# Where the conditioning loads and transpositions stand in the first mixer of a two-layer decoder trunk

## The chip, the cores and the metric

The kernel runs on one core of one Trainium2 chip. Its five engines work side by side, each through a queue of its own, in order: TensorE (PE) multiplies matrices and transposes, VectorE (DVE) and ScalarE (ACT) do elementwise work, GpSimd (POOL) and SyncE (SP) here mostly begin DMA transfers. An instruction waits in its queue for semaphores of other engines or of transfers, and everything behind it in that queue waits with it. The metric is the device time of one execution in microseconds.

## The reference

Two layers of a decoder trunk, for 256 tokens of width 1024, in fp32. Each layer takes six vectors of 1024 numbers from the conditioning vector `c`: a shift, a scale and a gate for the mixer and for the ConvFFN.

```python
cond = jax.nn.silu(c)
for layer in range(DEPTH):
    mod = cond @ ada_w[layer] + ada_b[layer]
    shift_m, scale_m, gate_m, shift_f, scale_f, gate_f = [m[:, None, :] for m in jnp.split(mod, 6, axis=-1)]
    h = rmsnorm(x, mix_pre_g[layer]) * (1.0 + scale_m) + shift_m
    if layer % 2 == 0:
        y = even_mixer(h, ab_w_in[i], ab_w_out[i], rel_bias)     # 8 MoBA heads "a", 8 dilated heads "b"
    else:
        y = odd_mixer(h, ...)                                    # latent attention, stick-breaking
    x = x + gate_m * rmsnorm(y, mix_post_g[layer])
    h = rmsnorm(x, ffn_pre_g[layer]) * (1.0 + scale_f) + shift_f
    y = conv_ffn(h, ffn_w_up[layer], ffn_conv_w[layer], ffn_conv_b[layer], ffn_w_down[layer])
    x = x + gate_f * rmsnorm(y, ffn_post_g[layer])
```

`even_mixer` multiplies `h` by `ab_w_in` into q, k, v of group a and of group b, adds a bias by distance to the scores of each head, takes softmaxes, and multiplies the heads' outputs by `ab_w_out`.

## The kernel before

Every fp32 product of weights and activations is made of three matmuls over a high and a low part. A weight tile is loaded (`load`, tag `raw`, four buffers), ScalarE casts its high part and VectorE subtracts it for the low part (`split`).

The first mixer runs in these stages. **Slices**: the inner dimension of 1024 is taken in four slices of 256. For each, the shift and scale of the mixer come from `ada_first` (its weights, `aw_first`, loaded by SP), `x` is transposed and conditioned, and q, k (`qk_mm`) and v (`v_mm`) of group a are accumulated. PE, DVE and ACT keep an order written out by hand here (`in_order`), up to `in_order.close()`. **Group a**: four pairs of heads (`attend`, tiles `sab`, `ltab`, `stab`, `oTab`). PE makes scores, VectorE adds the bias table `bt` and finds maxima (L590), ScalarE takes exponentials, VectorE scales (L601, L602), PE transposes (L604) and multiplies by v (L613, L616). **Projection b** (`qkv_proj`, tiles `psb`): weights `rawb_0`, `rawb_1` for q, the same names again for k, and `rawbv` for v. **Group b**, the same for the other eight heads, with tables of its own. **Output projection** (`y0m`), then the **first boundary**: gate, residual, norm, transposition, and the columns of scale and shift of the ConvFFN; then the ConvFFN of layer 0 (`u`), and layer 1.

The bias tables `bt` are read by SP out of `bias_d`, a table in DRAM that the kernel writes in the slices (L906), so `bt` waits for that write.

The other conditioning vectors are made in pieces of 512 columns beside this work. A piece is named by its first column among the 6144: 2048 and 2560 are the gate of the mixer, 3072 and 3584 the shift, 4096 and 4608 the scale, 5120 and 5632 the gate of the ConvFFN. Its four weight tiles `aw` (four buffers) are loaded by `ada_load`, all on POOL's queue. A piece of kind "p" is summed by PE (`ada_main`, 16 matmuls, L160). A piece of kind "v" is summed by VectorE (`ada_sum`, eight steps into `acc`, L207 and L205), in small steps handed out between other work by `step_aside`, and then transposed by four matmuls on PE (L177) and reduced by VectorE (`ada_keep`). In layer 0, 4096, 4608 and 3584 are of kind "v". `ADA_AT` says at which point each is requested: 2048 at "a0", 4096 at "a1", 2560 and 3072 at "a3", 4608 at "bv", 3584 at "b3". `gate_halves` starts the ConvFFN's gate at the boundary. Outside the hand-written order a scheduler sets each engine's order, by the order in which the code asks for things and by what each needs.

`tc.issue_after(...)` says behind which instruction a load may be put in its queue. A wait for a buffer that is still read is put in by the compiler. SP's transfers use eight semaphores in turn.

Of the kernel before, what the change touches and what calls it, by code (L numbers as in the profile page):

```python
# [17 lines left out]
P = 128  # L18
S = 256
D = 1024  # L20
# [23 lines left out]
    "dk": [("v", 1, 4, 1)],  # L44
    "d3": [("v", 1, 3, 1)],
}
BUFS = {"raw": 4, "whi": 4, "wlo": 4, "aw": 4, "gate": 2, "qkv": 8, "t": 13, "o": 8, "part": 2, "brow": 2,
        "ss": 4, "rstd": 4, "st": 4, "rp": 2, "kr": 2}


# [15 lines left out]
def trunk_kernel(  # L66
# [8 lines left out]
    nc = tc.nc  # L75
# [14 lines left out]
    def bank(name, tag="g"):  # L90
        return psum.tile([P, 512], F32, tag=tag, name=name, bufs={"g": 3, "a": 1}[tag])
# [43 lines left out]
    nc.vector.tensor_mul(cpad[:, :, 0], sil, cT)  # L135

    mods, last_load, last_gelu, last_full, last_h, last_down, last_low, last_main = {}, [], [], [], [], [], [], []
    last_rstd, last_slice, last_first = [], [], []

    def ada_load(layer, c0, tag="aw"):  # L140
        ws = []
        for u in range(4):
            w = tl(tag, [P, 2, 512], f"aw_{layer}_{c0}_{u}")
            with tc.issue_after(last_rstd[0].ins):
                last_load[:] = [nc.gpsimd.dma_start(  # L145
                    w, ada_w[layer, u * 256:(u + 1) * 256, c0:c0 + 512].rearrange("(k p) f -> p k f", p=P))]
            ws.append(w)
        return ws
# [22 lines left out]
    def ada_keep(layer, which, k0, ps, part, blocks, gain, per=4):  # L171

        n = len(blocks)
        dst = mods[layer, which][:, k0:k0 + n]
        cols = ps[:, blocks[0] * P:(blocks[-1] + 1) * P]
        for b in blocks:
            nc.tensor.transpose(ps[:, b * P:(b + 1) * P], part[:, b * P:(b + 1) * P], ident)  # L177
        nc.vector.tensor_reduce(dst, cols.rearrange("p (b j r) -> p b j r", j=per, r=P // per)[:, :, :, 0],
                                axis=mybir.AxisListType.X, op=ALU.add)
        b0 = layer * 48 + which * KT + k0  # L180
        nc.vector.tensor_add(dst, dst, vT[:, b0:b0 + n])
        if gain is not None:
            g0 = gain + layer * KT + k0
            nc.vector.scalar_tensor_tensor(dst, dst, 1.0, vT[:, g0:g0 + n], op0=ALU.add, op1=ALU.mult)

    aside = []

    def columns_for(layer, which):
        if (layer, which) not in mods:
# [2 lines left out]
    def step_aside(n=1):  # L192

        for _ in range(n):
            if aside:
                with tc.issue_after(last_low[0].ins):
                    if next(aside[0], aside) is aside:
                        aside.pop(0)
# [10 lines left out]
    def ada_vector(layer, which, h, gain):  # L209

        columns_for(layer, which)
        c0 = which * D + h * 512
        ws = ada_load(layer, c0)
        acc = small(f"acc_{layer}_{c0}", tag="part")
        yield from ada_sum(acc, ws)
        yield
        ada_keep(layer, which, 4 * h, bank(f"ada_{layer}_{c0}", "a"), acc, range(4), gain, P)

    def ada_cols(layer, which, h, gain=None):

# [31 lines left out]
    def ada_gate(layer, which, h, post_g, tag="aw", on="a", on_vector=False):  # L252

        c0 = which * D + h * 512
        ws = ada_load(layer, c0, tag)
        if (layer, which) not in mods:
            mods[layer, which] = tl("gate", [P, D], f"gate_{layer}_{which}")
            with tc.issue_after(last_load[0].ins):
                nc.gpsimd.dma_start(mods[layer, which], post_g[layer:layer + 1, :].broadcast_to([P, D]))
        g = mods[layer, which][:, h * 512:(h + 1) * 512]  # L260
        part = small(f"part_{layer}_{c0}", tag="brow")
        if on_vector:
            brow = small(f"brow_{layer}_{c0}", (1, 512), tag="t")
            nc.scalar.dma_start(brow, ada_b[layer:layer + 1, c0:c0 + 512])
            yield from ada_sum(part, ws)
            yield
            nc.vector.tensor_add(part[0:1, :], part[0:1, :], brow)
            ps = bank(f"ada_{layer}_{c0}", on)
            nc.tensor.matmul(ps, ones, part, start=True, stop=True)
            nc.vector.tensor_mul(g, ps, g)  # L270
            return
        nc.scalar.dma_start(part[P - 1:P, :], ada_b[layer:layer + 1, c0:c0 + 512])
        ps = bank(f"ada_{layer}_{c0}", on)
        yield
        ada_main(ps, ws, at_once=which == 2)
        yield
        nc.scalar.copy(part[0:P - 1, :], ps[0:P - 1, :])
        yield
        nc.tensor.matmul(ps, ones, part, start=True, stop=True)  # L279
        yield  # L280
        nc.vector.tensor_mul(g, ps, g)

    def gate_halves(which, layer, post_g):
        step_aside(99)
        halves = [ada_gate(layer, which, h, post_g, *on) for h, on in enumerate((("aw", "a"), ("qkv", "g")))]
        for h in halves:
            next(h)
        return halves
# [19 lines left out]

    def load(src, k, n, name):
        raw = tl("raw", [P, k, n], name)  # L310
        nc.sync.dma_start(raw, src.rearrange("(k p) f -> p k f", p=P))
        return raw

    def split(src, shape, name, aside=False, tags=("whi", "wlo")):
# [190 lines left out]
    def rows_of(w, u, c0, n, name):  # L505
        return load(w[u * 512:(u + 1) * 512, c0:c0 + n], 4, n, f"raw{name}_{u}")
# [10 lines left out]
                nc.scalar.copy(view, ps)  # L517
        return evac

    def qkv_proj(w, c0, name):  # L520

        q, k, v = qkv_tiles(name)
        list(qkv_steps(w, c0, name, q, k, v))
        return q, k, v

    def qkv_tiles(name):
        q, k, v = (qkv_tile(f"{n}{name}") for n in "qkv")
        return q, k, v.rearrange("p (t a) b -> p t (a b)", t=2)

    def qkv_steps(w, c0, name, q, k, v):  # L530
        for i, (dst, sc) in enumerate(((q, HD ** -0.5), (k, None))):
            ps = y_tile(f"ps{name}_{i}")
            for u in range(2):
                feat_mm([ps[:, 0, :], ps[:, 1, :]], rows_of(w, u, c0 + i * 512, 512, f"{name}{i}"), u, f"{name}{i}",
                        keep_feat(dst, sc) if u else None)
            more_ada(f"{name}{'qk'[i]}")
        yield
        ps = y_tile(f"ps{name}_v")
        for u in range(2):
            tok_mm([ps[:, 0, :], ps[:, 1, :]], rows_of(w, u, c0 + 1024, 512, f"{name}v"), u, 512, f"{name}v")  # L540
        keep_v(v, [ps[:, 0, :], ps[:, 1, :]])
        more_ada(f"{name}v")
# [248 lines left out]
    def slice_load(i):  # L791
        k0, n = SLICES[i]
        w = w_in[k0 * P:(k0 + n) * P]
        raw_qk[i] = tl("raw", [P, n, 1024], f"rawaqk_{i}")
        for k in range(n):
            nc.sync.dma_start(raw_qk[i][:, k, :], w[k * P:(k + 1) * P, 0:1024])
        raw_v[i] = tl("raw", [P, n, 512], f"rawav_{i}")
        last_slice[:] = [nc.sync.dma_start(raw_v[i], w[:, 1024:1536].rearrange("(k p) f -> p k f", p=P))]

    def slice_x(i, ts=range(2)):  # L800
        k0, n = SLICES[i]
# [118 lines left out]
        keep_feat(qkv[1])(half, pk[:, half, :])  # L920
    keep_v(qkv[2], pv)

    in_order.close()

    def pairs_ab(group, q, k, v):
# [4 lines left out]

    pairs = pairs_ab(0, *qkv)
    gs = attend(pairs, "a")
    qkv = qkv_proj(w_in, 1536, "b")
    gs += attend(pairs_ab(1, *qkv), "b")
    ys = y_tiles("y0m")
    out_proj(ys, ab_w_out[0], gs[0:4], True, False, "o0a")
# [215 lines left out]
```

## Time and profile before

| what | value |
|---|---|
| time, median of three runs | 699.66 us (698.59 to 701.04) |
| the profiled execution | 697.84 us, of which its span is 695.9 us |
| PE busy | 658.0 us, 95% of the span, 4541 matmuls |
| DVE busy | 526.7 us, 76% |
| ACT busy | 368.6 us, 53% |
| POOL busy | 95.2 us, 14% |
| DMA | 159.10 MB, 229 GB/s over the span |

Times in the rows are microseconds from the start of the span. A row of the timeline gives start, length, engine, line, operation, output and inputs, how many instructions it joins, and in brackets how long the engine had been idle before it and what ended that. PEclk is the TensorE clock that was granted, as a share of full speed. "q1 hardware_dynamic" is the queue of the transfers begun by SP (and ACT), "q0 software_dynamic" of those begun by POOL.

### The profile page before, as it was taken

To read this page: it belongs to the slowest core of one execution; us is meant where nothing else is said; L and a number is where in the kernel's file an instruction comes from. 1 tells how busy PE (TensorE), PEld (TensorE's weight loads), DVE (VectorE), ACT (ScalarE), POOL (GpSimd) and SP (SyncE) were. 2 spreads that over 40 slices of the span, in tenths; PEclk is the share of its full clock that TensorE was granted. 3 is DMA by queue.
4 is the path that set the end of the run, shared out by engine and by line. 5 is a ranking of instruction groups with operands and counts; after the bars stand their busy time and mean duration, and the time that the engine had idled before them with its cause. 6 is when DMAs were issued, how large, how long until landed. Compare 5 with 4: busy or idle time off the path is not lost.

```text
span 695.9 us, 11779 instructions
## 1 busy us (share of the span) xinstructions
PE 658.0 (95%) x4541; PEld 573.1 (82%) x4541; DVE 526.7 (76%) x1007; ACT 368.6 (53%) x644; POOL 95.2 (14%) x180
## 2 busy tenths in 40 slices
PE   7978999489999999999998999999999999999996
PEld 6856886367699999999996997767699999999994
DVE  2443784685889999999997886874788777777775
ACT  3323754454675555455655644785465555555552
POOL 2020212230301011111124012631200000000000
PEclk9998999879999999999999999999999999999999
DMA  9999987995578878778894858723256655555611
GB/s 312 295 378 253 368 298 248 301 307 209 178 243 269 259 261 303 257 260 287 270 340 142 303 184 295 224 85 108 90 182 211 200 195 182 182 182 183 187 55 61
DMA packets 90466, 159.10 MB, mean 229 GB/s; under 512 B 4087, under 2 KB 62483, under 8 KB 90411
## 3 DMA queue, kind: packets, MB, share of 16 engines
q1 hardware_dynamic: 78259, 114.24, 49.7%
q0 software_dynamic: 12128, 44.11, 18.7%
q8 instruction: 35, 0.57, 0.3%
q14 instruction: 20, 0.16, 0.1%
q10 hardware_dynamic: 24, 0.02, 0.0%
HBM read 156.52 MB, written 1.84 MB: 228 GB/s over the span
## 4 chain that ended last, share of the span: by engine, by line
PE 80%; DMA 9%; DVE 4%; ACT 3%; POOL 1%; issue 1%; SPq 0%; DVEq 0%; POOLq 0%; ACTq 0%
PE u L480 35%; PE y1f L701 9%; PE y0f L701 8%; DMA aw_first<-in_ada_w 5%; PE psb L480 3%; PE psd L480 3%; PE y0m L701 2%; PE y1m L701 2%; DMA rawav<-in_ab_w_in 2%; DMA bt<-bias_d 2%; PE ada L160 1%; PE sab L604 1%; PE ada_first L160 1%; ACT junknm L338 1%; PE sab L613 1%
## 5 line engine op out<-in xcount | busy, mean ns | idle before, releaser
L145 POOL DMA_DIRECT2D aw<-in_ada_w x80 | 58.2, 729 | 333.1 <-DVE acc L205 181.6
L750 ACT ACTIVATE cv<-u,cvT 128x256 f32<-128x256 f32 x88 | 49.2, 561 | 65.6 <-PE u L480 61.7
L480 PE MATMUL u<-hh,wu_0h 128*128 128x256 f32 x352 | 69.9, 280 | 1.4 <-DVE hh L434 1.4
L480 PE MATMUL u<-hh,wu_1h 128*128 128x256 f32 x352 | 70.1, 280 | 0.0
L480 PE MATMUL u<-hh,wu_1l 128*128 128x256 f32 x352 | 69.9, 279 | 0.0
L480 PE MATMUL u<-hh,wu_0l 128*128 128x256 f32 x352 | 69.5, 279 | 0.0
L318 ACT CAST wu_1h<-rawu 128x1024 fp32r<-128x1024 f32 x44 | 46.3, 1051 | 31.1 <-PE y1f L701 17.6
L751 DVE SCALAR_TENSOR_TENSOR cv<-u,cvT,cv 128x255 f32<-128x255 f32 x88 | 42.0, 478 | 27.1 <-ACT cv L750 27.0
L205 DVE SCALAR_TENSOR_TENSOR acc<-aw,cpad,acc 128x512 f32<-128x512 f32 x77 | 58.2, 756 | 1.7 <-DMA aw<-in_ada_w 1.3
L480 PEld LDWEIGHTS u<-hh,wu_0h 128*128 128x128 f32 x352 | 54.7, 188 | 4.4 <-PE ada L279 3.0
L319 DVE TENSOR_TENSOR wu_0l<-rawu,wu_0h 128x1024 fp32r<-128x1024 f32 x44 | 53.6, 1221 | 5.3 <-ACT wu_0h L318 5.3
L318 ACT CAST wu_0h<-rawu 128x1024 fp32r<-128x1024 f32 x44 | 46.0, 1046 | 19.1 <-PE u L480 19.1
L319 DVE TENSOR_TENSOR wu_1l<-rawu,wu_1h 128x1024 fp32r<-128x1024 f32 x44 | 53.6, 1217 | 3.0 <-ACT wu_1h L318 2.9
L480 PEld LDWEIGHTS u<-hh,wu_1l 128*128 128x128 f32 x352 | 53.7, 188 | 0.0
L480 PEld LDWEIGHTS u<-hh,wu_1h 128*128 128x128 f32 x352 | 53.7, 188 | 0.0
L480 PEld LDWEIGHTS u<-hh,wu_0l 128*128 128x128 f32 x352 | 53.5, 188 | 0.0
L480 PE MATMUL u<-hl,wu_1h 128*128 128x256 f32 x352 | 48.2, 279 | 0.0
L480 PE MATMUL u<-hl,wu_0h 128*128 128x256 f32 x352 | 48.2, 279 | 0.0
L318 ACT CAST wd_0h<-rawd 128x1024 fp32r<-128x1024 f32 x26 | 27.3, 1048 | 35.3 <-PE u L480 31.8
L480 PEld LDWEIGHTS u<-hl,wu_1h 128*128 128x128 f32 x352 | 44.2, 188 | 0.0
L480 PEld LDWEIGHTS u<-hl,wu_0h 128*128 128x128 f32 x352 | 44.2, 188 | 0.0
L753 DVE SCALAR_TENSOR_TENSOR cv<-u,cvT,cv 128x254 f32<-128x254 f32 x88 | 41.8, 477 | 1.4
(561 smaller groups left out, 1564.8 us busy)
## 6 DMA issues: line engine op xcount, KB each, us to landing
rawu<-in_ffn_w_up SPq DMA_DIRECT2D x44, 1024.0 KB, 7.3
aw<-in_ada_w POOLq DMA_DIRECT2D x80, 512.0 KB, 6.2
rawd<-in_ffn_w_down SPq DMA_DIRECT2D x22, 1024.0 KB, 4.9
aw_first<-in_ada_w SPq DMA_DIRECT2D x32, 256.0 KB, 6.6
rawaqk<-in_ab_w_in SPq DMA_DIRECT2D x8, 512.0 KB
rawb<-in_ab_w_in SPq DMA_DIRECT2D x4, 1024.0 KB, 10.1
rawd<-in_cd_w_in SPq DMA_DIRECT2D x4, 1024.0 KB, 6.3
rawc<-in_cd_w_in SPq DMA_DIRECT2D x4, 544.0 KB
```

What stands on the lines that cost most here:

```text
L145: last_load[:] = [nc.gpsimd.dma_start(w, ada_w[layer, u * 256:(u + 1) * 256, c0:c0 + 512].rearrange("(k p) f -> p k f", p=P))]
L160: last_main[:] = [nc.tensor.matmul(ps[32 * j:32 * j + 32, 0:cols], cpad[:, k, :], ws[k // 2][:, k % 2, 0:cols], start=(n < 4), stop=(n >= ...
L205: nc.vector.scalar_tensor_tensor(acc, w, c_k, acc, op0=ALU.mult, op1=ALU.add)
L318: nc.scalar.copy(hi, src)
L319: low = nc.vector.tensor_tensor(lo, src, hi.bitcast(F32), op=ALU.subtract)
L338: nc.scalar.activation(junk, src, AF.Square, scale=D ** -0.5, accum_out=ss)
L480: nc.tensor.matmul(dst(f), w[:, k, f * P:(f + 1) * P], h[:, 4 * u + k, :], start=(u == 0 and first(f) and f not in seen), stop=(u == 1 and ...
L604: nc.tensor.transpose(self.ps[j][:, b * P:(b + 1) * P], lt[:, b * P:(b + 1) * P], ident)
L701: last_down[:] = [nc.tensor.matmul(ys[t][:, h, :], g[p // 2][:, t * P:(t + 1) * P], wu[p % 2][:, h * 512:(h + 1) * 512], start=start and p ...
L750: nc.scalar.activation(tt[:, s, :], u_ps, AF.Identity, bias=cvT[:, bcol:bcol + 1], scale=col(2))
L751: nc.vector.scalar_tensor_tensor(tt[:, s, 1:S], u_ps[:, 0:S - 1], col(1), tt[:, s, 1:S], op0=ALU.mult, op1=ALU.add)
L753: nc.vector.scalar_tensor_tensor(tt[:, s, 2:S], u_ps[:, 0:S - 2], col(0), tt[:, s, 2:S], op0=ALU.mult, op1=ALU.add)
```

## The change

Four things move. (1) The first half of the mixer's gate of layer 0 (the piece 2048, and the tile `gate_2` with the norm's weights) is loaded by SP, behind the latest `raw` load, instead of by POOL behind the start's norm. (2) The first two weight loads of projection b (`raws_b`) are begun before the hand-written order ends, and handed to `qkv_proj`. (3) The transpositions and the reduction of VectorE's sums of layer 0 are kept as functions, and asked for at the start of `gate_halves` instead of right behind their sum. (4) The buffers of the tag `part`, which hold such sums, are three instead of two.

```diff
-BUFS = {"raw": 4, "whi": 4, "wlo": 4, "aw": 4, "gate": 2, "qkv": 8, "t": 13, "o": 8, "part": 2, "brow": 2,
+BUFS = {"raw": 4, "whi": 4, "wlo": 4, "aw": 4, "gate": 2, "qkv": 8, "t": 13, "o": 8, "part": 3, "brow": 2,
...
-            with tc.issue_after(last_rstd[0].ins):
-                last_load[:] = [nc.gpsimd.dma_start(
+            queue, behind = (nc.sync, last_raw) if (layer, c0) == (0, 2 * D) else (nc.gpsimd, last_rstd)
+            with tc.issue_after(behind[0].ins):
+                last_load[:] = [queue.dma_start(
...
-        ada_keep(layer, which, 4 * h, bank(f"ada_{layer}_{c0}", "a"), acc, range(4), gain, P)
+        keep = lambda: ada_keep(layer, which, 4 * h, bank(f"ada_{layer}_{c0}", "a"), acc, range(4), gain, P)
+        if layer:
+            keep()
+        else:
+            kept.append(keep)
...
-                nc.gpsimd.dma_start(mods[layer, which], post_g[layer:layer + 1, :].broadcast_to([P, D]))
+                (nc.gpsimd if last_load[0].ins.engine == mybir.EngineType.Pool else nc.sync).dma_start(
+                    mods[layer, which], post_g[layer:layer + 1, :].broadcast_to([P, D]))
...
     def gate_halves(which, layer, post_g):
         step_aside(99)
+        while kept:
+            kept.pop(0)()
...
         raw = tl("raw", [P, k, n], name)
-        nc.sync.dma_start(raw, src.rearrange("(k p) f -> p k f", p=P))
+        last_raw[:] = [nc.sync.dma_start(raw, src.rearrange("(k p) f -> p k f", p=P))]
...
-    def qkv_steps(w, c0, name, q, k, v):
+    def qkv_steps(w, c0, name, q, k, v, raws=()):
+        raws = list(raws)
...
-                feat_mm([ps[:, 0, :], ps[:, 1, :]], rows_of(w, u, c0 + i * 512, 512, f"{name}{i}"), u, f"{name}{i}",
+                raw = raws.pop(0) if raws else rows_of(w, u, c0 + i * 512, 512, f"{name}{i}")
+                feat_mm([ps[:, 0, :], ps[:, 1, :]], raw, u, f"{name}{i}",
...
+    raws_b = [rows_of(w_in, u, 1536, 512, "b0") for u in range(2)]
     in_order.close()
...
-    qkv = qkv_proj(w_in, 1536, "b")
+    qkv = qkv_proj(w_in, 1536, "b", raws_b)
```

SP's queue before, from the write of the bias table to the loads of k's weights; `rawaqk` and `rawav` are the weights of the last slice:

```order
L906 DMA bias_d<-bias 512x1x384
L796 DMA rawaqk_437<-in_ab_w_in 128x1024 x2
L798 DMA rawav_440<-in_ab_w_in 128x2x512
L311 DMA rawb_0_1005<-in_ab_w_in 128x4x512
L837 DMA bt_442<-bias_d 32x4x256 x4
L837 DMA bt_447<-bias_d 32x4x256 x4
L311 DMA rawb_1_1063<-in_ab_w_in 128x4x512
L311 DMA rawb_0_1125<-in_ab_w_in 128x4x512
L311 DMA rawb_1_1183<-in_ab_w_in 128x4x512
```

The same stretch of SP's queue with the change:

```order
L917 DMA bias_d<-bias 512x1x384
L807 DMA rawaqk_437<-in_ab_w_in 128x1024 x2
L809 DMA rawav_440<-in_ab_w_in 128x2x512
L848 DMA bt_442<-bias_d 32x4x256 x4
L848 DMA bt_447<-bias_d 32x4x256 x4
L320 DMA rawb_0_701<-in_ab_w_in 128x4x512
L320 DMA rawb_1_703<-in_ab_w_in 128x4x512
L146 DMA aw_2048_0_774<-in_ada_w 128x2x512
L146 DMA aw_2048_1_776<-in_ada_w 128x2x512
L146 DMA aw_2048_2_778<-in_ada_w 128x2x512
L146 DMA aw_2048_3_780<-in_ada_w 128x2x512
L265 DMA gate_2_782<-in_mix_post_g 128x1024
```

The eight `bt` loads now stand ahead of both loads of q's weights, and the five loads of the gate's first half, which were the first of POOL's queue, stand behind these.

PE before, at the end of the slices and the start of group a (`psa_v` is v of group a, `sab` are scores):

```order
L328 MATMUL psa_v_165<-wav_3h,hl 128x512
L160 MATMUL ada_2048_782<-aw_2048_3_776,cpad 32x512 x2
L160 MATMUL ada_2048_782<-aw_2048_2_774,cpad 32x512 x2
L160 MATMUL ada_2048_782<-aw_2048_1_772,cpad 32x512 x2
L160 MATMUL ada_2048_782<-aw_2048_0_770,cpad 32x512 x2
L582 MATMUL sab_0_1_703<-ka,qa 128x128
L582 MATMUL sab_1_1_724<-ka,qa 128x128
```

PE there with the change:

```order
L337 MATMUL psa_v_165<-wav_3h,hl 128x512
L593 MATMUL sab_0_1_707<-ka,qa 128x128
L593 MATMUL sab_1_1_728<-ka,qa 128x128
L593 MATMUL sab_1_0_727<-ka,qa 128x128
L595 MATMUL sab_1_1_728<-ka,qa 128x256
L595 MATMUL sab_1_0_727<-ka,qa 128x256
L489 MATMUL psb_0_999<-hh,wb_0_0h 128x256 x2
L489 MATMUL psb_0_999<-hh,wb_0_0l 128x256 x2
L489 MATMUL psb_0_999<-hh,wb_0_0h 128x256 x2
L489 MATMUL psb_0_999<-hh,wb_0_0l 128x256
L161 MATMUL ada_2048_786<-aw_2048_3_780,cpad 32x512 x2
L161 MATMUL ada_2048_786<-aw_2048_2_778,cpad 32x512
```

The piece 2048 moved behind five scores and seven matmuls of projection b.

VectorE before, ahead of the bias tables of group b:

```order
L319 TENSOR_TENSOR wo0a_1l<-rawo0a_1542,wo0a_1h 128x1024
L207 TENSOR_SCALAR acc_4608_1333<-aw_4608_0_1325,cpad 128x512
L205 SCALAR_TENSOR_TENSOR acc_4608_1333<-aw_4608_0_1325,cpad,acc_4608_1333 128x512
L205 SCALAR_TENSOR_TENSOR acc_4608_1333<-aw_4608_1_1327,cpad,acc_4608_1333 128x512
L319 TENSOR_TENSOR wo0a_0l<-rawo0a_1576,wo0a_0h 128x1024
L205 SCALAR_TENSOR_TENSOR acc_4608_1333<-aw_4608_1_1327,cpad,acc_4608_1333 128x512
L178 TENSOR_REDUCE mod_3_971<-ada_3072_980 128x4
L181 TENSOR_TENSOR mod_3_971<-mod_3_971,vT 128x4
L319 TENSOR_TENSOR wo0a_1l<-rawo0a_1576,wo0a_1h 128x1024
L205 SCALAR_TENSOR_TENSOR acc_4608_1333<-aw_4608_2_1329,cpad,acc_4608_1333 128x512
L319 TENSOR_TENSOR wo0c_0l<-rawo0c_1620,wo0c_0h 128x1024
L205 SCALAR_TENSOR_TENSOR acc_4608_1333<-aw_4608_2_1329,cpad,acc_4608_1333 128x512
```

VectorE there with the change (`bt_1307` is the first table of group b):

```order
L328 TENSOR_TENSOR wo0c_0l<-rawo0c_1604,wo0c_0h 128x1024
L601 ISA ltab_0_0_1339,stab_0_0_1340<-sab_0_0_1330,bt_1307 128x128
L601 ISA stab_0_0_1340 128x1
L601 ISA ltab_0_0_1339,stab_0_0_1340<-sab_0_0_1330,bt_1307 128x256
L601 ISA stab_0_0_1340 128x1
L601 ISA ltab_0_1_1345,stab_0_1_1346<-sab_0_1_1331,bt_1307 128x128
L601 ISA stab_0_1_1346 128x1
L601 ISA ltab_0_1_1345,stab_0_1_1346<-sab_0_1_1331,bt_1307 128x256
L601 ISA stab_0_1_1346 128x1
L209 TENSOR_SCALAR acc_4608_1325<-aw_4608_0_1317,cpad 128x512
L601 ISA ltab_1_0_1364,stab_1_0_1365<-sab_1_0_1355,bt_1307 128x128
L601 ISA stab_1_0_1365 128x1
```

Before, seven of the eight steps of `acc_4608` stood ahead of the first table. With the change the first step stands behind the first pair of scores, and the seven others behind the second. On PE the 16 matmuls of the piece 3072, whose `aw` buffers the loads of 4608 take, move from the middle of `psb_v` to behind its last matmul and the first score of group b; the four transpositions of 4608 move from ahead of group b's first L604 to behind the transpositions of its third pair, and those of 3584 to ahead of the transpositions of its last pair. The order behind the first boundary is as before.

## Rows read from the trace of the kernel before

**Rows 1.** Windows: stretch and length, busy (count) by engine, PEclk, DMA, GB/s:

```profile
54.50:58.30 3.80, 3.73 (x17) 1.06 (x17) 0.00 (x0) 0.00 (x0) 0.00 (x0) 0.50 0.94 226
58.30:73.70 15.40, 15.40 (x105) 14.18 (x104) 10.30 (x14) 8.93 (x12) 0.00 (x0) 0.97 0.93 270
73.70:130.00 56.30, 56.30 (x416) 43.96 (x414) 37.40 (x91) 31.75 (x68) 12.27 (x17) 1.00 0.85 306
130.00:142.70 12.70, 1.35 (x7) 0.72 (x4) 10.97 (x33) 5.37 (x19) 2.17 (x3) 0.67 1.07 296
142.70:172.20 29.50, 29.49 (x149) 22.27 (x150) 20.37 (x59) 13.85 (x35) 7.19 (x11) 0.91 0.80 268
```

**Rows 2.** Timeline of PE, the fourth slice's conditioning:

```profile
54.57 3.75 PE L160 MATMUL ada_first<-aw_first,cpad 128*32 128x512 f32 x16 [5.09 <-DMA aw_first<-in_ada_w]
```

**Rows 3.** Chain of waits, pieces by start and length:

```profile
74.00 1.85 PE ada L160 x16
75.86 0.53 PE sab L582 x5
...
78.10 1.36 PE psb L480 x10
```

**Rows 4.** DMA view, 42.5 to 52.5 us, all packets and the two queues:

```profile
DMA packets 1888, 3.80 MB, mean 380 GB/s; under 512 B 147, under 2 KB 1248, under 8 KB 1888
...
q0 software_dynamic: 720, 2.62, 69.4%
q1 hardware_dynamic: 1168, 1.18, 35.2%
...
rawaqk<-in_ab_w_in SPq DMA_DIRECT2D x2, 512.0 KB
bias_d<-bias SPq DMA_DIRECT2D x1, 768.0 KB
rawav<-in_ab_w_in SPq DMA_DIRECT2D x1, 512.0 KB
```

**Rows 5.** DMA view, 58.5 to 68.5 us, the rate in 40 parts, and the issues:

```profile
GB/s 352 360 328 344 311 377 377 393 401 385 426 410 410 410 410 377 385 389 234 229 201 197 176 139 213 193 209 213 221 213 201 160 209 205 176 164 193 115 102 98
DMA packets 1767, 2.73 MB, mean 273 GB/s; under 512 B 144, under 2 KB 940, under 8 KB 1765
...
bt<-bias_d SPq DMA_DIRECT2D x8, 128.0 KB, 9.7
```

**Rows 6.** Timeline of PE at group b:

```profile
119.74 1.92 PE L160 MATMUL ada<-aw,cpad 128*32 128x512 f32 x16
...
127.81 0.49 PE L582 MATMUL sab<-kb,qb 64*128 64x128 f32 x4
...
139.11 1.09 PE L177 MATMUL ada<-ident,acc 128*128 128x128 f32 x4 [8.85 <-DVE acc L205]
142.71 3.11 PE L604 MATMUL sab<-ident,ltab 128*128 128x128 f32 x12 [2.51 <-DVE ltab L601]
...
155.74 0.60 PE L177 MATMUL ada<-ident,acc 128*128 128x128 f32 x4
```

**Rows 7.** Timeline of POOL, its loads of 4608:

```profile
121.11 2.89 POOL L145 DMA_DIRECT2D aw<-in_ada_w  x4 [10.61 <-PE ada L160]
```

**Rows 8.** Timeline of SP, group b's tables:

```profile
122.60 12.44 SPq L837 DMA_DIRECT2D bt<-bias_d  x8
```

**Rows 9.** Timeline of VectorE at group b:

```profile
125.66 0.49 DVE L207 TENSOR_SCALAR acc<-aw,cpad 128x512 f32<-128x512 f32 x1 [3.51 <-DMA aw<-in_ada_w]
...
137.10 0.29 DVE L590 CUSTOM_DVE_ANT_0 ltab<-sab,bt 128x128 f32<-128x128 f32 x1 [1.64 <-DMA bt<-bias_d]
...
138.22 0.75 DVE L205 SCALAR_TENSOR_TENSOR acc<-aw,cpad,acc 128x512 f32<-128x512 f32 x1
...
151.79 0.74 DVE L205 SCALAR_TENSOR_TENSOR acc<-aw,cpad,acc 128x512 f32<-128x512 f32 x1
```

**Rows 10.** Tile aw, 100 to 135 us:

```profile
DMA to landing us min/median/max: 4.5/7.1/9.0
```

More of the change, by code (lines that the diff above doesn't have):

```diff
@@ L137, in trunk_kernel @@
     mods, last_load, last_gelu, last_full, last_h, last_down, last_low, last_main = {}, [], [], [], [], [], [], []
-    last_rstd, last_slice, last_first = [], [], []
+    last_rstd, last_raw, last_first = [], [], []
     def ada_load(layer, c0, tag="aw"):
@@ L184, in ada_keep @@
             nc.vector.scalar_tensor_tensor(dst, dst, 1.0, vT[:, g0:g0 + n], op0=ALU.add, op1=ALU.mult)
-    aside = []
+    aside, kept = [], []
     def columns_for(layer, which):
@@ L518, in keep_feat, with qkv_proj @@
         return evac
-    def qkv_proj(w, c0, name):
+    def qkv_proj(w, c0, name, raws=()):
         q, k, v = qkv_tiles(name)
-        list(qkv_steps(w, c0, name, q, k, v))
+        list(qkv_steps(w, c0, name, q, k, v, raws))
         return q, k, v
@@ L797, in slice_load @@
         raw_v[i] = tl("raw", [P, n, 512], f"rawav_{i}")
-        last_slice[:] = [nc.sync.dma_start(raw_v[i], w[:, 1024:1536].rearrange("(k p) f -> p k f", p=P))]
+        nc.sync.dma_start(raw_v[i], w[:, 1024:1536].rearrange("(k p) f -> p k f", p=P))
     def slice_x(i, ts=range(2)):
```

## The prediction

> **What bounds the kernel now.** I read the page first: PE is busy for 95% of the span, so a gain has to come from the places where PE stands still or runs slowly. The windows name two of them in the first mixer. From 54.5 to 58.3 us PE is busy but at a granted clock of 0.50, the lower of its two levels (1.2 of 2.4 GHz), and from 130.0 to 142.7 us it does 1.35 us of work in 12.70. Between and behind, in 58.3 to 130 and 142.7 to 172.2, it is full [rows 1]. So a shift that is won before 58.3 is carried whole to 130.
>
> The timeline says who ends these two waits. At 54.57 PE had waited 5.09 us for the transfer of `aw_first`, the weights of the last slice's conditioning, and then took 3.75 us for its 16 matmuls [rows 2], where 16 of the same kind at the full clock take 1.85 [rows 3]. The DMA view of 42.5 to 52.5 us shows what kept that transfer: the engines are full at 380 GB/s, and POOL's queue moves 2.62 MB of 3.80 in that time, SP's 1.18 [rows 4]. POOL's bytes are the gate's first half, which PE first uses at 74.00 [rows 3].
>
> The second place begins when PE has made the scores of group b. It waits 8.85 us for the last step of the sum 4608, transposes that, and waits 2.51 us more for the softmax of the first pairs [rows 6]. VectorE in turn took a step of that sum ahead of the tables, waited for `aw` until 125.66, and reached the first table at 137.10 after waiting for `bt` [rows 9]. Those tables were begun at 122.60 [rows 8], beside the four `aw` loads of POOL from 121.11 [rows 7].
>
> **The change part by part.**
>
> *The gate's load leaves the early stage.* At 380 GB/s the 2.62 MB are 6.9 us of all engines. Without them the last `aw_first`, which ended PE's wait at 54.57, is there 6.9 us sooner, by 47.7. PE came for it at 54.57 - 5.09 = 49.5. So the 5.09 us go. If PE doesn't stand, its clock has no reason in these rows to fall, and the 3.75 us become 1.85, 1.9 less. Together 7.0 us. What is late next is the last slice's `rawaqk` and `rawav`, on the same queue behind `aw_first`; they come forward by the same 6.9 us, so I cost them at nothing. If the clock stays low, 5.1 remain.
>
> *The gate's load on SP's queue.* It now stands behind the bias table, `rawaqk`, `rawav`, eight tables and two loads of q's weights. I add up from 47.7. The bias table has 768 KB, at 226 GB/s, the rate of the stretch in which it ran [rows 1, 4]: 3.5 us. `rawaqk` and `rawav` have 1.57 MB, at 380: 4.1. The tables have 8 x 128 KB; the right half of the rates of 58.5 to 68.5 shows about 200 GB/s, where tables made up the queue [rows 5]: 5.2. Two `rawb` of 1 MB at 380: 5.5. Four `aw` of 512 KB: 5.5. Sum 23.8, so the gate's weights land at 71.5. PE wants them at 74.00 - 7.0 = 67.0, plus five scores of 0.53 in all and seven matmuls of 0.136 each [rows 3], so at 68.5. A new wait of 3.0 us, then. Behind it stand all of group a and projection b. With everything at 380 the weights land at 67.7 and there is no wait; with everything at the mean of 273 [rows 5] it is 75.5 and the wait is 7.0, all that was won. I take 3.0, since its parts are each read from the stretch that resembles them. What reaches 130 is X = 4.0, with ends 7.0 and 0.
>
> The rule that speaks against this part: the Trainium skill, DMA: Bandwidth & Descriptors, section "Queues, rings and completion order", says that a DMA engine goes round between the queues that have work, and takes one queue's descriptors in ring order. The counts of 720 and 1168 packets side by side [rows 4] agree with the sharing; that the gate's load would wait its turn on one queue no run here shows yet, and by it the wait is that of the sum above rather than none.
>
> *The weights of q earlier, the tables ahead of them.* No bytes are added. The loads of q's first weights are needed by the seven matmuls ahead of 2048, and are two transfers ahead of it in the queue: they are covered by the same wait. POOL loses five issues in the early stage; its next load waits for the buffers that 2048 frees, as before.
>
> *The transpositions and the sum 4608.* The order shows three moves at group b: the tables of the first pair are ahead of the sum's first step, the 16 matmuls of 3072 are behind `psb_v`, and the transpositions of 4608 don't stand ahead of the first pair any more. So the 8.85 us for the sum go. What is late next? VectorE still has the first step of 4608 ahead of the second pair, and it needs the first `aw` of 4608. That load waits for the matmuls of 3072. PE reaches these at 127.81 - 1.85 - 4.0 = 122.0 [rows 3, 6]; from their start to POOL's issue it was 121.11 - 119.74 = 1.4 [rows 6, 7], from there to VectorE's first step 4.55 [rows 7, 9]. So the step runs at 128.0. The tables were begun at 122.60 and now at 118.6; 1 MB at 200 GB/s and the issues end at about 125, so the `aw` come last. From a step of the sum beside the tables to PE's first L604 it was 142.71 - 138.22 = 4.5 [rows 6, 9], with the same work between. So L604 starts at 132.5, 10.2 us earlier than 142.71. The moved matmuls cost nothing there: PE stands anyway.
>
> From L604 to the transpositions of 3584 it was 155.74 - 142.71 = 13.0 [rows 6]; now PE comes there at 145.5, and with 4608's 0.6 us in between at 146. The sum 3584 must be done by then. From 4608's first step to its last it was 138.22 - 125.66 = 12.6 [rows 9]: 140.6. The last load of 3584 takes the buffer that this frees, 7.1 us to landing [rows 10], and two steps of 0.75 [rows 9]: 149.2. PE waits 3.2 us. The ends: no wait, if both sums run faster beside fewer transfers; and 154.8, if from the issue of 4608 to the end of 3584 it takes the 31.4 us of before (121.11 to 152.5) [rows 7, 9]. I take 149.2, which is the sum of single rows. From 155.74 to 172.2 it was 16.5 [rows 1, 6], and nothing was moved out of that. So the output projection ends at 165.7 instead of 172.2: 6.5 us won.
>
> *The third `part` buffer* only keeps a sum alive longer; it costs 2 KB per partition and no time. Behind the boundary PE is as full as before, and the ConvFFN's first weights are begun earlier by the same shift. I carry the 6.5 us to the end.
>
> **The sum.** 697.84 - 6.5 = 691.3 us for the profiled execution, which stands 1.82 us under the median of the runs shown; for the median 693.1. By X alone this moves one for one: X = 7.0 gives 690.0, X = 0 gives 697.1.
>
> **The rivals.**
>
> *A, the sums bind.* From POOL's issue of 4608 to the end of 3584 the chain keeps its 31.4 us, since each load waits for a buffer that a step frees. For it: VectorE is busy 10.97 of 12.70 us there and 20.37 of the next 29.50 [rows 1], and each step is queued among other work. Against it: part of the length was waiting for transfers that shared the engines with the tables. With X = 4.0 PE waits until 154.8, the projection ends at 171.3, and 0.9 us are won: 698.8.
>
> *B, slower.* The same chain, begun later. The loads of 4608 started at 121.11 because 3072 stood in the middle of `psb_v`; now they start at 127.4 - X. If the chain keeps its length, the projection ends at 175.3 - X, so below X = 3.1 the kernel loses. That is when the gate's weights land later than 72.4, less than a microsecond behind my sum. At X = 0.5, it ends at 174.8, 2.6 later: 702.3. For it: 273 GB/s was the mean of the stretch with the tables [rows 5]. Against it: as for A.
>
> *C, more.* The sum 3584 is ready when PE comes at 146: the projection ends at 162.5, 9.7 us earlier, 689.9.
>
> *D, nothing.* The same bytes pass the same engines, and the engines are full in 42.5 to 58.3, so what the first wait gives, the second takes, X = 0, and A's middle ground leaves 0 to 2.5. The Trainium skill has this as a rule (DMA: Bandwidth & Descriptors, "Issuing engines are not separate DMA queues": transfers of all issuing engines run on the same 16 and interleave). The trace agrees as to the shared rate [rows 4], but 2.62 MB that are needed at 68 and not at 49 are a change of order, not of the issuing engine. About 698.5.
>
> **How the numbers follow.** Differences under 0.3%, 2.1 us, can't be told from no change. My forecast with X from 1 to 7 and the second wait between its ends 0.60: faster, in its own range of 690 to 697.3. C 0.08: faster. A and D together 0.21: a quarter of it faster, most the same. B 0.11: slower. Faster 0.60 x 0.97 + 0.08 + 0.05 = 0.71; slower 0.11 and a little of A, 0.12; the same 0.17. The range leaves out B's end and the best of C: 689.5 to 699.6.
>
> **What would show it.** In the profile after: no wait at the last slice's `ada_first`, its 16 matmuls at about 1.9 us, `psa_v` ending near 67; a wait of about 3 us at the 16 matmuls of 2048, ended by a transfer on SP's queue; PE full to about 126; one wait before L604 that ends near 132.5, put down to VectorE behind the `aw` of 4608; one at the transpositions of 3584 of about 3 us; the ConvFFN starting near 177.5 instead of 184. I am wrong at the first step if the clock or the wait stays at 50 us, at the second if 2048 waits over 5 us, at the third if PE waits at 3584 until about 155.

## The result, and the profile after

The changed kernel takes 694.19 us (median of 8 runs, 692.01 to 696.59), the kernel before 699.37 us beside it (8 runs, 697.98 to 701.04): a ratio of 0.9927, 95% interval 0.9904 to 0.9949. Predicted was 693.1 us. The profiled execution took 693.43 us with a span of 691.5, so 4.4 us less than before. The total came near; the way there was another than predicted, and that is what the rest is about. The medians differ by 5.2 us, the two traces, of one execution each, by 4.4.

The windows of the changed kernel, cut so that each holds the work of one window of before (stretch, length, busy time and count of PE, PEld, DVE, ACT, POOL, then PEclk, DMA, GB/s):

```profile
48.70:65.80 17.10, 17.10 (x122) 14.21 (x120) 7.69 (x13) 6.88 (x9) 0.00 (x0) 1.00 1.05 306
65.80:78.40 12.60, 8.96 (x43) 4.16 (x42) 8.00 (x23) 6.14 (x14) 1.84 (x3) 0.73 1.05 389
78.40:129.30 50.90, 50.90 (x369) 40.87 (x369) 33.37 (x75) 28.98 (x62) 9.95 (x14) 1.00 0.84 280
129.30:135.70 6.40, 1.43 (x8) 0.79 (x5) 4.22 (x20) 3.65 (x16) 0.72 (x1) 0.90 1.03 356
135.70:164.70 29.00, 27.71 (x140) 19.99 (x141) 24.05 (x68) 12.71 (x32) 8.52 (x12) 0.90 0.95 319
```

The same work stood before in these windows:

```profile
49.40:73.90 24.50, 19.41 (x121) 15.24 (x120) 10.82 (x15) 9.13 (x12) 0.00 (x0) 0.86 0.95 277
73.90:79.00 5.10, 5.10 (x44) 3.02 (x44) 3.23 (x9) 3.53 (x8) 2.88 (x4) 1.00 1.05 390
79.00:130.00 51.00, 51.00 (x373) 40.94 (x372) 34.16 (x83) 28.02 (x61) 9.40 (x13) 1.00 0.83 297
142.70:169.40 26.70, 26.69 (x137) 19.93 (x137) 18.64 (x56) 12.51 (x32) 6.32 (x9) 0.90 0.83 278
```

Read the lengths in pairs. The last slice lasts 17.1 us instead of 24.5, and it begins 0.7 sooner: 8.1 won by 65.8. The start of group a takes 12.6 instead of 5.1: 7.5 lost, so that at the end of projection b the kernel is 0.7 ahead. The wait at group b is 6.4 instead of the 12.70 of [rows 1]: 6.3 won. The output projection's stretch takes 29.0 instead of 26.7: 2.3 lost. Sum 4.7; the first matmul of the ConvFFN starts at 179.36 instead of 184.01, and behind that the two are alike. So the early gain was given back almost whole, and nearly all that is left arose at group b.

**Where the early gain went.** PE of the changed kernel, last slice and start of group a, answering to [rows 2, 3]:

```profile
48.76 1.92 PE L161 MATMUL ada_first<-aw_first,cpad 128*32 128x512 f32 x16
...
65.52 0.40 PE L337 MATMUL psa_v<-wav_3h,hl 128*128 128x512 f32 x1
68.61 0.57 PE L593 MATMUL sab<-ka,qa 64*128 64x128 f32 x5 [2.69 <-DVE qa L524]
...
72.46 1.93 PE L161 MATMUL ada<-aw,cpad 128*32 128x512 f32 x6 [0.95 <-DMA aw<-in_ada_w]
...
75.90 2.15 PE L161 MATMUL ada<-aw,cpad 128*32 128x512 f32 x10
```

The early wait is gone, and the 16 matmuls run at the full clock. Then PE waits twice, and the 16 matmuls of 2048, now in two pieces, take 1.93 and 2.15 us instead of 1.85 together [rows 3]. The window's clock is 0.73: from 69.6 to 76.4 it is 0.50, the lower of the two levels, behind a stretch from 65.9 to 68.6 in which PE had been idle. Waits of 2.69 and 0.95 and 3.9 us more of busy time for the same work (8.96 against 5.10) are the 7.5 us. From the first matmul of 2048 to the next of projection b it is 5.9 us:

```profile
72.50:78.40 5.90, 5.90 (x25) 1.81 (x25) 2.39 (x17) 1.69 (x7) 1.84 (x3) 0.67 1.05 388
```

How much of that is the lower clock shows in e1 below, which has the same order there.

The first of the two waits was not foreseen. VectorE there:

```profile
65.50 2.36 DVE L328 TENSOR_TENSOR wb_0l<-rawb,wb_0h 128x1024 fp32r<-128x1024 f32 x2 [3.83 <-ACT wb_0h L327]
67.78 1.28 DVE L524 TENSOR_SCALAR qa<-psa_q 128x512 f32<-128x512 f32 x2
```

The weights of projection b are loaded earlier, so their split was put ahead of the evacuation of q of group a (`qa`), and VectorE stood 3.83 us for it. The Trainium skill, PSUM — Partial Sum Buffer, section "Engine vs sequencer instructions", says that VectorE's queue is strictly first in, first out. These rows agree: `psa_q` was complete before, and `qa` still ran behind `wb_0l`.

**Where the gain arose.** SP and POOL at group b, answering to [rows 7, 8]; first SP, then POOL:

```profile
120.81 5.47 SPq L848 DMA_DIRECT2D bt<-bias_d  x8
```

```profile
126.33 2.89 POOL L146 DMA_DIRECT2D aw<-in_ada_w  x4 [12.49 <-PE ada L161]
```

The eight table loads pass in 5.47 us instead of 12.44. POOL's loads of 4608, which had started 1.5 us ahead of them, start 5.5 us behind, because the matmuls of 3072, whose buffers they take, moved behind `psb_v`. VectorE, answering to [rows 9]:

```profile
128.50 0.28 DVE L601 CUSTOM_DVE_ANT_0 ltab<-sab,bt 128x128 f32<-128x128 f32 x1
...
131.87 0.49 DVE L209 TENSOR_SCALAR acc<-aw,cpad 128x512 f32<-128x512 f32 x1 [2.18 <-DMA aw<-in_ada_w]
...
135.38 0.28 DVE L612 TENSOR_SCALAR ltab<-ltab,stab 128x128 f32<-128x128 f32 x1
...
153.07 0.74 DVE L207 SCALAR_TENSOR_TENSOR acc<-aw,cpad,acc 128x512 f32<-128x512 f32 x1
```

The first table is 8.6 us earlier, and the first scaling (L612), which PE's first L615 needs, stands behind the first step of the sum, which waits for its load, and behind a second step and a weight split. PE, answering to [rows 6]:

```profile
134.39 1.09 PE L178 MATMUL ada<-ident,acc 128*128 128x128 f32 x4 [4.75 <-DVE mod L179]
135.72 0.95 PE L615 MATMUL sab<-ident,ltab 128*128 128x128 f32 x3 [0.24 <-DVE ltab L612]
...
153.96 0.63 PE L178 MATMUL ada<-ident,acc 128*128 128x128 f32 x4 [0.29 <-DVE mod L182]
```

The wait of 4.75 looks like the bound, but the scaling of 135.38 would have held L615 until about 135.7 in any case. The last row is the transposition of 3584: almost no wait.

### The profile page after: what moved, and what is told of

It is laid out like the page before. It is cut to its first block, busy times and chain, and to the rows that moved or that the text cites. A ratio compares the mean times of both kernels' runs of the same rounds, so it can differ in the third digit from the quotient of the medians.

```text
span 691.5 us, 11776 instructions
## 1 busy us (share of the span) xinstructions
PE 660.6 (96%) x4541; PEld 573.3 (83%) x4541; DVE 526.2 (76%) x1007; ACT 369.0 (53%) x644; POOL 91.8 (13%) x175
## 4 chain that ended last, share of the span: by engine, by line
PE 76%; DMA 10%; DVE 4%; issue 4%; ACT 3%; POOL 2%; SPq 0%; POOLq 0%; DVEq 0%; ACTq 0%
PE u L489 36%; PE y1f L712 9%; PE y0f L712 8%; DMA aw<-in_ada_w 5%; PE psd L489 3%; DMA aw_first<-in_ada_w 3%; PE y1m L712 2%; PE psb L489 2%; DMA rawav<-in_ab_w_in 2%; PE y0m L712 1%; PE ada L161 1%; PE psa_q L829 1%; ACT junknm L347 1%; PE psa_k L829 1%; PE sd L655 1%
## 5 line engine op out<-in xcount | busy, mean ns | idle before, releaser
L146 POOL DMA_DIRECT2D aw<-in_ada_w x76 | 55.4, 729 | 334.2 <-DVE acc L207 179.0
```

The source lines that it names most:

```text
L146: last_load[:] = [queue.dma_start(w, ada_w[layer, u * 256:(u + 1) * 256, c0:c0 + 512].rearrange("(k p) f -> p k f", p=P))]
```

## The experiments

Ten kernels, each with its ratio to the kernel before run beside it. The theory of e1 to e4 was that the early gain is lost in group a, and that the saving at group b needs the moved transpositions. From e5 on it was that the gain at group b comes of two orders, the tables' loads ahead of those of 4608, and VectorE's tables ahead of the sum 4608. The rival was that the relieved early stage carries the gain. In the diffs `...` stands for lines left out.

**e1 and e2: each half alone.** e1 has the loads (parts 1 and 2), without the kept transpositions; e2 the kept transpositions, with the gate on POOL's queue. Against the changed kernel:

```diff
e1
-BUFS = {... "part": 3, ...
+BUFS = {... "part": 2, ...
-        keep = lambda: ada_keep(...)
...
+        ada_keep(layer, which, 4 * h, bank(f"ada_{layer}_{c0}", "a"), acc, range(4), gain, P)
e2
-            queue, behind = (nc.sync, last_raw) if (layer, c0) == (0, 2 * D) else (nc.gpsimd, last_rstd)
+            queue, behind = (nc.gpsimd, last_rstd)
-    raws_b = [rows_of(w_in, u, 1536, 512, "b0") for u in range(2)]
-    qkv = qkv_proj(w_in, 1536, "b", raws_b)
+    qkv = qkv_proj(w_in, 1536, "b")
```

> Only the loads: the gate's first half on SP and the two early weight loads; the transpositions of VectorE's sums stay where they were, two part buffers. Theory: what the early stage wins (7.4 us, 49.4 to 65.8) is given back in group a (PE waits for qa and for the gate's weights), so at 129 us PE stands as with the full change, 0.7 us ahead of before; the saving at group b needs the moved transpositions. Near 699 us, within 1.5 us of before. Rival 1: the loads bring group b's tables and sums earlier by themselves, and the whole gain of about 5 us shows here (694). Rival 2: the early gain of 7 us reaches the end (692).

> Only the moved transpositions and the third part buffer; the gate's first half stays on POOL, the weight loads of q where they were. Theory: the early wait of 5.1 us stays and nothing is given back in group a; at group b the first L604 no longer waits for the transpositions of 4608, but VectorE still has six steps of that sum ahead of the first table, so part of the saving at most: 1 to 3 us, 696.5 to 698.5. Rival: the transpositions are all that matters, the full 4 to 5 us show here (694.5 to 695.5).

e1: 698.83 us, 0.9996 (0.9980 to 1.0012). e2: 699.89 us, 1.0021 (1.0004 to 1.0038). Neither half gains anything; for e1 that was expected, for e2 it was not (696.5 to 698.5). In both, the matmuls of 3072 stay in the middle of `psb_v` (they start at 120.64 and 118.94). Only with both halves did the scheduler move them; why isn't shown. In e1 the early wait is gone as with the whole change, and the tables' loads take 5.40 us; but VectorE's order has five steps of the sum ahead of the first table, and these wait for loads. VectorE of e1:

```profile
129.88 0.49 DVE L209 TENSOR_SCALAR acc<-aw,cpad 128x512 f32<-128x512 f32 x1 [4.43 <-DMA aw<-in_ada_w]
...
136.39 0.28 DVE L597 CUSTOM_DVE_ANT_0 ltab<-sab,bt 128x128 f32<-128x128 f32 x1
```

PE of e1 then stands as long as before:

```profile
141.93 0.95 PE L611 MATMUL sab<-ident,ltab 128*128 128x128 f32 x3 [12.96 <-DVE ltab L608]
```

In e2 the loads of 4608 begin at 120.30, the tables behind them take 12.41 us, and the first table runs at 136.40.

e1 also tells what the lower clock was worth in group a. PE of e1, and the window that answers to 72.50:78.40 above:

```profile
69.35 0.57 PE L589 MATMUL sab<-ka,qa 64*128 64x128 f32 x5 [2.24 <-DVE qa L520]
73.19 1.06 PE L161 MATMUL ada<-aw,cpad 128*32 128x512 f32 x6 [1.72 <-DMA aw<-in_ada_w]
75.03 1.90 PE L161 MATMUL ada<-aw,cpad 128*32 128x512 f32 x10
```

```profile
73.20:77.30 4.10, 4.10 (x25) 1.35 (x25) 2.16 (x15) 1.70 (x7) 1.84 (x3) 1.00 1.05 389
```

The same two waits are there, the same 25 matmuls, and the granted clock stayed at 1.00; it did so in e5 too. So of the 5.9 us of the changed kernel's trace 1.8 are the lower clock, which this execution got and two others with the same order did not.

**e3: `qa` ahead of the split.** The changed kernel, with the split of q's first weights put behind the evacuations of group a's q and k:

```diff
...
+        behind = name.startswith("wb0")
-        with tc.issue_after(last_full[0].ins) if aside else nullcontext():
+        with tc.issue_after(last_full[0].ins) if aside else tc.issue_after(last_k[0].ins) if behind else nullcontext():
             nc.scalar.copy(hi, src)
-        low = nc.vector.tensor_tensor(lo, src, hi.bitcast(F32), op=ALU.subtract)
+        with tc.issue_after(last_q[0].ins) if behind else nullcontext():
+            low = nc.vector.tensor_tensor(lo, src, hi.bitcast(F32), op=ALU.subtract)
...
```

> The full change, with VectorE's qa and ScalarE's ka queued ahead of the split of q's first weights. Theory: PE's wait of 2.7 us at the first scores of group a goes, but the gate's weights land at 72.4 as before and PE comes to them sooner, so the wait there grows from 0.9 to about 3.5 us; net 1 to 2 us better than the full change, 692 to 693. Rival: the queue of VectorE was the binder, all of 2.7 us and the slow clock behind it come back: 4 us or more better, 690 or less.

694.49 us, 0.9944 (0.9925 to 0.9963): the same as the changed kernel, where 692 to 693 was expected. The wait for `qa` is gone, and its time is found in front of the gate's weights. PE of e3:

```profile
73.14 2.47 PE L161 MATMUL ada<-aw,cpad 128*32 128x512 f32 x16 [3.45 <-DMA aw<-in_ada_w]
```

So it is the landing of the gate's weights (72.46 in the changed kernel, 73.14 here) that sets the end of this stretch; the wait for `qa` lay within it.

**e4 and e6: work for PE until the gate's weights land.** e4 is the changed kernel, with the first half of projection b's q asked for ahead of group a; e6 also puts the first low parts of k's weights behind the tables of group a's second pair.

```diff
e4
...
+    qkv = qkv_tiles("b")
+    steps = qkv_steps(w_in, 1536, "b", *qkv, raws_b, early=True)
+    next(steps)
     gs = attend(pairs, "a")
-    qkv = qkv_proj(w_in, 1536, "b", raws_b)
+    list(steps)
e6, besides
...
+        with tc.issue_after(soft["ab0_1", 1].ins) if name.startswith("wb1_0_0") else nullcontext():
+            low = nc.vector.tensor_tensor(lo, src, hi.bitcast(F32), op=ALU.subtract)
```

> The full change, with the first half of projection b's q (48 matmuls, 5.6 us) asked for ahead of group a, so PE has it while qa, the tables and the gate's weights come. Theory: PE works from about 66.8, comes to the gate's matmuls at about 73.5, when their weights have landed; the 7.5 us given back between 65.8 and 78.4 shrink to about 1, and if group b's wait doesn't grow, 5 to 6 us better than the full change, 688 to 689. Rival: group b waits for the tables and the sum 4608 at a fixed time, and takes back what is won: no better than 693.

> The kernel with projection b's q asked for early (e4), and the low parts of k's first weights queued on VectorE behind the tables of group a's second pair. Theory: in e4 VectorE stood until 76.7 for k's first weights with the tables of group a behind it, and PE waited 3.25 us at 81.7; that wait goes, and 1.5 to 3 us more are won: 689 to 690.5. Rival: group b's start is set by a fixed time of its tables and sums, and takes back what comes earlier: 692, as e4.

e4: 692.02 us, 0.9926 (0.9897 to 0.9955), where 688 to 689 was expected. Both waits near 70 are gone, and a new one stands at 81.72, behind VectorE, which waits for the weights of k. PE and VectorE of e4:

```profile
81.72 0.33 PE L617 MATMUL sab<-ident,ltab 128*128 128x128 f32 x1 [3.25 <-DVE ltab L614]
```

```profile
76.69 2.36 DVE L328 TENSOR_TENSOR wb_0l<-rawb,wb_0h 128x1024 fp32r<-128x1024 f32 x2 [6.07 <-ACT wb_0h L327]
```

e6: 689.43 us, 0.9880 (0.9853 to 0.9907), as expected. That wait goes too; one of 2.5 us for ScalarE comes in its place. The medians fall by 2 and 5 us against the changed kernel, but a gain is not shown by these two alone: e4's ratio is the changed kernel's 0.9927, and e6's interval still touches that of the changed kernel (from 0.9904).

**e5 and e7: the order of the sum.** Both ask for 4608 one pair later and put the first step of its sum behind the scaling of group b's second pair: e5 in the changed kernel, e7 in the kernel before.

```diff
-    "bv": [("v", 0, 4, 1)],
+    "b1": [("v", 0, 4, 1)],
...
+            if after in scaled:
+                with tc.issue_after(scaled.pop(after).ins):
+                    nc.vector.tensor_scalar_mul(acc, ws[0][:, 0, :], cpad[:, 0, 0:1])
+                continue
...
```

> The full change, with the first step of VectorE's sum 4608 queued behind the scaling of group b's second pair of heads (and 4608 asked for one pair later). Theory: VectorE no longer waits 2.18 us for the weights of 4608 between the tables of the first and second pair, nor does the step there; PE's first L604-kind transposition of group b moves from 135.7 to about 132.5, and unless the later sums then hold PE, the kernel is 1.5 to 3 us better than the full change: 691 to 692.5. Rival: the sums 4608 and 3584, begun later, hold PE at their transpositions, and nothing is left: 694 or more.

> The kernel before, with nothing of the change, but the first step of the sum 4608 queued behind the scaling of group b's second pair (4608 asked for one pair later). Theory: what the change won at group b has two parts, VectorE's order, and tables that land at 128 instead of 136 because the loads of 4608 begin behind them. Here only the first is had: the tables still land at 136, L604 starts near 140 instead of 142.7, 2 to 3 us won: 696 to 697. Rival: VectorE's order is the whole of it, 5 us: 694. Rival: the tables' landing is the whole of it, no gain: 699.

e5: 689.18 us, 0.9869 (0.9851 to 0.9886), better than the 691 to 692.5 expected; L620, the first transposition of a softmax, starts at 130.78 instead of the changed kernel's 135.72. e7: 695.81 us, 0.9952 (0.9935 to 0.9970), just under what was expected, since there the tables' loads still take 11.50 us. PE of e5 and VectorE of e7:

```profile
130.78 0.81 PE L620 MATMUL sab<-ident,ltab 128*128 128x128 f32 x4 [2.85 <-DVE ltab L617]
```


```profile
135.01 0.29 DVE L595 CUSTOM_DVE_ANT_0 ltab<-sab,bt 128x128 f32<-128x128 f32 x1 [4.12 <-DMA bt<-bias_d]
```

**e9 and e10: the two orders without the change.** Both start from the kernel before. e10 only asks for 3072 one point later, so that its matmuls stand behind `psb_v`; e9 has that and the order of e7.

```diff
-    "a3": [("p", 0, 2, 1), ("p", 0, 3, 0)],
-    "bv": [("v", 0, 4, 1)],
e10
+    "a3": [("p", 0, 2, 1)],
+    "bv": [("p", 0, 3, 0), ("v", 0, 4, 1)],
e9, with the lines of e7
+    "a3": [("p", 0, 2, 1)],
+    "bv": [("p", 0, 3, 0)],
+    "b1": [("v", 0, 4, 1)],
```

> The kernel before, with none of the four moves of the change. Two orders are altered: the piece 3072 is asked for where projection b's v is, so that its 16 matmuls stand behind psb_v and the loads of 4608 begin behind the tables bt; and the first step of the sum 4608 stands behind the scaling of group b's second pair, 4608 being asked for one point later. My theory, that the whole gain arises at group b and comes of these two orders, whichever queue the gate is loaded on: the first wait of 5 us at ada_first stays; bt takes about 5.5 us instead of 12.4, group b's first table runs near 128.5 instead of 137.1, the first transposition of a softmax near 132 instead of 142.7; u near 175; 690 us (688.5 to 691.5). The rival, that the tables come early only if the early stage has been relieved by moving the gate's load: bt as before, first table near 135, 694 us or more.

> The kernel before, with one edit: the piece 3072 is asked for one point later (where projection b's v is), so that its 16 matmuls stand behind psb_v; none of the four moves of the change. VectorE then has one step of the sum 4608 ahead of the first pair's tables and one ahead of the second pair's. My theory: this one placement gives most of what the full change gave, since that came of the tables' arrival and of their place ahead of the sum: bt takes about 5.5 us, but the first step of the sum still waits for its load ahead of the tables, so the first table runs near 131; 695 us (693.5 to 696.5). The rival, that the moved gate load or the kept transpositions are needed: 698 to 700 us.

e10: 694.50 us, 0.9948 (0.9927 to 0.9968). e9: 689.66 us, 0.9875 (0.9855 to 0.9894). Both came as the theory had it. One entry of the table gives 3.5 us where the whole change gave 5.2 (the intervals overlap), and both orders give what they gave on top of the change in e5. SP and VectorE of e10:

```profile
120.48 5.46 SPq L837 DMA_DIRECT2D bt<-bias_d  x8
```

```profile
131.04 0.48 DVE L207 TENSOR_SCALAR acc<-aw,cpad 128x512 f32<-128x512 f32 x1 [3.79 <-DMA aw<-in_ada_w]
131.44 0.28 DVE L590 CUSTOM_DVE_ANT_0 ltab<-sab,bt 128x128 f32<-128x128 f32 x1
```

The tables' loads pass as fast as with the change, but the first step of the sum still stands ahead of the first table. The early wait is still there in e9, and the tables come early all the same. PE, SP, POOL and VectorE of e9, in that order:

```profile
54.26 3.29 PE L162 MATMUL ada_first<-aw_first,cpad 128*32 128x512 f32 x16 [3.27 <-DMA aw_first<-in_ada_w]
...
132.91 2.87 PE L610 MATMUL sab<-ident,ltab 128*128 128x128 f32 x12 [3.92 <-DVE ltab L607]
```

```profile
121.36 5.42 SPq L843 DMA_DIRECT2D bt<-bias_d  x8
```

```profile
125.46 2.88 POOL L147 DMA_DIRECT2D aw<-in_ada_w  x4 [16.19 <-PE ada L162]
```

```profile
129.00 0.29 DVE L596 CUSTOM_DVE_ANT_0 ltab<-sab,bt 128x128 f32<-128x128 f32 x1 [0.88 <-PE ada L179]
```

That settles the rival: the loads on SP's queue and the kept transpositions aren't needed for the gain.

**e8: the best of them.** e5 and e6 in one kernel, so the changed kernel with both orders and the earlier q.

> The full change, with q early, k's first weights behind the tables of group a, and the sum 4608 behind the scaling of group b (e4, e5 and e6 together). If the gains are of different waits they add up: 687 to 689. If group b's tables are at a fixed time: 691 to 692.

685.92 us, 0.9825 (0.9805 to 0.9844), faster than both kernels and than the 687 to 689 expected. PE's waits from 36 to 190 us in e8 (who waits, for whom, total, times, longest):

```profile
PE ada L291 <- ACT part L289: 3.0, 1, 3.0
PE sab L624 <- DVE ltab L621: 2.6, 1, 2.6
PE ada_first L162 <- DMA aw_first<-in_ada_w: 1.1, 1, 1.1
```

e8 is 3.3 us under e5 (689.18), and the two intervals don't touch, so the early q and k's later weights pay on top of both orders. Where they pay, the kept traces don't show. The first matmul of the ConvFFN, in e5 and then in e8:

```profile
173.16 0.50 PE L494 MATMUL u<-hh,wu_0h 128*128 128x256 f32 x2 [0.68 <-DVE hh L448]
173.72 0.50 PE L495 MATMUL u<-hh,wu_0h 128*128 128x256 f32 x2 [0.68 <-DVE hh L449]
```

The traced e8 is not ahead there. It is also the slowest of its four runs (688.57; the others 685.33 to 686.06), and e5's trace is 1.4 us longer behind that point, with a granted clock of 0.72 from 454.9 to 461.0 where e8 had 1.00. So it is argued, not shown, that the 3.3 us come of PE having other work until the gate's weights land. e8 without the early loads wasn't run either, so whether those are needed for them is open.

## Why the prediction was right or wrong

*The early wait: right.* 7.0 us were predicted, 7.4 came in that stretch, and 0.7 before it, where the two slices before waited 1.8 us in all instead of 2.6. `psa_v` ended at 65.9, predicted 67.0.

*The new wait at 2048: the mechanism right, the size wrong.* This is the step of the prediction that failed: "I take 3.0 [...] What reaches 130 is X = 4.0". X was 0.7. The sum along SP's queue was good, 71.5 against a start at 72.46. But PE was there earlier: 65.9 and the same five scores and seven matmuls make 67.4 instead of 68.5, so the weights cost 5.0 us and not 3.0. And the matmuls behind the wait ran partly at the lower clock, which the sum had left out: 5.9 us against e1's 4.1 for the same 25, so 1.8. 5.0 + 1.8 are 6.8 of the 7.5; the rest was not taken apart. The prediction had counted 1.9 us as won because an early wait and its slow clock vanish, and had not asked what the clock does behind the wait that takes its place. Here it fell, in e1 and e5 it did not, so the 1.8 us are bad luck of this execution; the 5.0 are not: in e1 it is 4.6, from 68.6 (`psa_v` ending at 67.11, and the same scores and matmuls) to 73.19. The wait for `qa` was missed as well, but e3 shows that it cost nothing by itself.

*The order at group b: right in kind.* The 8.85 us for the sum went, the tables ran early, and the next thing was the first step of 4608 ahead of the second pair, as predicted. L615 came at 135.72, not 132.5: X was 3.3 smaller, so PE reached 3072's matmuls at 124.96 instead of 122.0, and the load took 5.5 us to VectorE's step instead of 4.55; from there to PE it was 3.9 instead of 4.5. The prediction named both orders, but gave them no value of their own: the 10.2 us were theirs and X's together. e9 and e10 show that the orders stand without X.

*The sum 3584: its end was sized right from a wrong start, and the wait was not there.* From the first step of 4608 to the last of 3584 it took 131.87 to 153.07, 21.2 us, just as predicted (128.0 to 149.2). Of the wait of 3.2 us, 0.3 came, since "nothing was moved out of" the 16.5 us was wrong: 36 matmuls of `y0m` stand ahead of that transposition instead of 24, and PE came to it 18.2 us behind its first L615, where the prediction had 13.5. So the tail was 29.0 us (135.7 to 164.7), 2.3 longer than before, where the prediction had 3.7 longer.

*The sum.* 6.5 us were forecast and 4.65 came by the start of the ConvFFN: 3.2 less because L615 was late, 1.4 more because the tail was shorter. Errors of opposite sign brought the total near: that was luck.

*The rivals.* A and B did not come: the chain of both sums, 31.4 us before, took 27.5 from POOL's issue at 126.33 to its last step, and X fell below the 3.1 from which B was to decide, without a loss. C had the small wait at 3584 right, but not what stands ahead of it. D was right for the early stage, X being 0.7, and wrong for group b. It failed there because the tables' loads and those of 4608 were put in another order, and that was worth more than the bytes tell.

## What to carry to other kernels

A wait that is removed at a transfer can come back at the next one on the same queue, as it did here, unless the engine has other work until that lands: ask for such work along with the load. In e8 that came with 3.3 us, by the medians. When a change has several parts, list what each engine's order does far from the place of the edit, and price those moves alone; here placements that the scheduler shifted as a side effect were nearly the whole gain. And where a wait is added, price what stands behind it at both levels of the clock: here the same matmuls took 5.9 us in one trace and 4.1 in another.

## What the runs showed of the hardware

- Eight loads of 128 KB out of the table in DRAM took SP 5.31 to 6.45 us in eight kernels in which the four loads on POOL's queue began behind them (after, e1, e3, e5, e6, e8, e9, e10), and 11.50 to 12.44 us where four loads of 512 KB had begun about 1.5 us ahead (before, e2, e7). The Trainium skill, DMA: Bandwidth & Descriptors, section "Queues, rings and completion order", says that a DMA engine goes round between the queues with work; the longer times agree with sharing. In e4 they took 9.95 us, though POOL's loads of 4608 began 7.4 us behind them. There the loads of the piece before, 3072, had begun shortly ahead of the tables, from 113.41 on; in the eight kernels the last of these had begun 5.5 us or more ahead. SP and POOL of e4:

```profile
117.30 9.95 SPq L850 DMA_DIRECT2D bt<-bias_d  x8
```

```profile
113.41 2.88 POOL L146 DMA_DIRECT2D aw<-in_ada_w  x4 [10.47 <-PE ada L161]
```

  So e4 agrees with sharing as well. Why a start 1.9 us ahead, as in e1, is enough for the short time stays open.
- With POOL's queue empty, 42.5 to 52.5 us after the change moved 2.56 MB instead of the 3.80 of [rows 4]. The rate was 98 to 135 GB/s for about 4.5 us, with the engines shown as full (the last line is the queue's share):

```profile
GB/s 344 344 352 352 340 356 352 340 352 354 383 377 344 309 123 117 117 117 117 104 98 104 98 98 98 98 98 131 131 115 125 135 354 432 410 426 410 418 426 418
...
q1 hardware_dynamic: 1717, 2.56, 100.8%
```

  Next in SP's queue behind `aw_first` is the write of the bias table; that it was this which ran there is read from the queue's order and not shown. If it was, the prediction's 226 GB/s for that write was twice too high. A share of full engines did not tell here that they moved many bytes.
